# Linear attention of a two-block layer stack: two heads walked block by block, in an order fixed for TensorE

## The chip, the cores and the metric

The kernel runs on one core of one Trainium2 chip. The metric is the device time of one execution in microseconds (us). In the rows PE is TensorE's matmul, PEld its weight load, DVE is VectorE, ACT is ScalarE, POOL is GpSimd and SP is SyncE, which issues the transfers. L708 is line 708 of the kernel before.

## What is computed

The program is a stack of two blocks on 512 tokens of 1024 features: a first block with a gated linear attention (GLA) layer and a sparse attention layer, and a second block of a hybrid layer with adaptive modulation. The change touches the linear attention alone, which runs from some 20 to some 220 us. It has 4 heads with keys of 128 and values of 256, and goes over the tokens in chunks of 64 with a state:

```python
q_e = q * jnp.exp(b)              # b: running sum of the log decay in a chunk
k_e = k * jnp.exp(-b)
k_d = k * jnp.exp(b_last - b)
a = jnp.where(causal, jnp.einsum('bhnid,bhnjd->bhnij', q_e, k_e), 0.0)
o_intra = jnp.einsum('bhnij,bhnjv->bhniv', a, v)
def step(state, xs):
    o = jnp.einsum('bhcd,bhdv->bhcv', qe, state)
    state = dec[..., None] * state + jnp.einsum('bhcd,bhcv->bhdv', kd, vc)
    return state, o
...
o = rms_norm(o, head_norm)
o = o.transpose(0, 2, 1, 3).reshape(B, S, GLA_V) * jax.nn.silu(z)
return o @ w_out.astype(jnp.float32)
```

q, k, v, z and the decay's input are projections of the same normalised activations. Two small parts of other blocks are computed beside it: the modulation of the second block, `silu(c) @ w_ada`, and the table of angles for the rotary positions of the sparse attention.

## The kernel before, in words

**Tiles.** The two chunks of 64 make a block of 128 tokens; there are `NB` = 4 blocks to a head. Every projection is exact in three products of split operands: activations and weights are each a high part and a low part (`hH`, `hL`, and `w_hi`, `w_lo`), and high x high, high x low and low x high are summed. ScalarE copies out a weight's high part (L149) and VectorE makes the low part (L150), in halves of 128 x 1024; activations are split in the same way (L356, L357). A projection with features on the partitions (`proj_feat`, L236 to L238) is 24 matmuls of 512 columns; one with tokens on the partitions (`proj_toks`, L287 to L289) is 24 matmuls of 256 columns for each block of tokens.

**One head.** `gla_q` projects the queries and scales them by the decay on VectorE (L658, two halves, and L662). `gla_k` makes two scaled sets of keys, `kk` (L685, L686) and `kb` (L687, L688). `gla_v` writes the values (L605) into `gv`, one tile of [128, 4, 256] for a head, in two buffers. `gla_core` goes over the four blocks: scores (L708) go from PSUM through VectorE's copies (L711, L712) into one of two tiles `aT`, which GpSimd masks (L713); the product with the values, and with the state of the block before (L716, L718), is squared and summed on ScalarE (L720) and copied on VectorE to `on` (L721); the keys are transposed (L724), copied by ScalarE to `kt` (L726), and give the state's increment (L728, L731, L733). Behind the fourth block come the mean of squares (L736), a reciprocal root in three rounds of Newton's method on VectorE (L298 to L307, steps of 128 x 4), and GpSimd scales the four blocks of `on` by it (L739). `gla_gate` then transposes `on` (L749, 8 transposes, in two halves) and multiplies it with `silu(z)` (L745, L751).

**What lies between.** `gla_z` projects z for a head (two projections of 24 matmuls each, multiplied out at L696). `ada(n)` advances the modulation by n steps: a step issues the transfer of 512 KB of `w_ada` into one of two tiles `wada` (L548) and multiplies it on VectorE with a row sum (L549). `rope_tables` makes the angle table: steps on VectorE of 128 x 512 (L510 to L530, the later ones once for the sine and once for the cosine), then a sine on ScalarE (L531). It takes one value of `ON[2]` first (L510), and so comes no earlier than head 2's scaling.

**The order.** The heads go in two pairs (`g` = 0, 1). The code emits: queries of both heads, keys of both heads with two ada steps behind each, the whole core of the first head, two ada steps, the whole core of the second. Behind the first pair come the gates of heads 0 and 1 and the values of heads 2 and 3; behind the second pair the remaining ada steps, the z projections of heads 2 and 3, the rope table and the gates of heads 2 and 3. Then the output projection of the linear attention follows, whose input is what the gates wrote, split into `hH` and `hL` (L356, L357). In this stage the code's order is not the order on the engines: a scheduler orders the instructions of every engine, TensorE's among them, by its own estimates. Other stages of the kernel already hold TensorE to the order of the code, with `in_order(True)` (L182). An engine works through its queue in order, so what waits at the head of the queue holds up what is behind it. PSUM tiles come from four tags with 2, 3, 2 and 1 buffers:

```python
BANKS = {"pj": 2, "sc": 3, "tr": 2, "pv": 1}
```

## Time and profile before

| what | value |
|---|---|
| median of 3 runs | 1243.33 us (1241.85 to 1245.09) |
| the profiled execution's own time | 1242.91 us |
| its span in the trace | 1241.2 us |
| mean granted TensorE clock | 0.987 |
| busy: PE | 1186.5 us, 96% of the span |
| busy: DVE | 798.3 us, 64% |
| busy: ACT | 626.2 us, 50% |
| busy: POOL | 274.4 us, 22% |
| chain that ended last | PE 65%, DVE 12%, ACT 8%, issue 6%, DMA 5%, POOL 3% |

The span is the time from the first to the last recorded instruction; the execution's own time has 1.7 us more around it. Busy shares are of the whole span and say nothing of a single stage, for which the windows are read. The granted clock is the share of full speed at which TensorE was let run, and stands for two levels, 1.2 and 2.4 GHz: a stretch at 1.00 ran at the upper one. The rows of a timeline give the start, the length and the instruction; in square brackets stands the time for which the engine was idle before it, and whose work ended that time. A list of waits sums such idle times by who waited and for whom.

### The profile page before, as it was taken

What the parts mean: (1) busy time and instruction counts of PE and PEld (TensorE: products, weight loads), DVE (VectorE), ACT (ScalarE), POOL (GpSimd) and SP (SyncE); (2) the same over time, 40 slices, a digit from 0 to 9 for tenths busy, and PEclk for the clock granted to TensorE, in tenths of its full rate; (3) what the DMA queues carried; (4) which work ended last, traced back from release to release, by engine and by line L of the source; (5) the groups of instructions that cost most, each with busy time, mean ns of one, the idle gap of its engine ahead of it and who ended that gap; (6) DMA issues with size and microseconds to landing.
All of it is one profiled execution on the core that took longest, in us unless ns stands there. A gap on an engine that the chain in (4) does not pass through costs nothing.

```text
span 1241.2 us, 18591 instructions
## 1 busy us (share of the span) xinstructions
PE 1186.5 (96%) x6880; PEld 1009.8 (81%) x6880; DVE 798.3 (64%) x1534; ACT 626.2 (50%) x1308; POOL 274.4 (22%) x398
## 2 busy tenths in 40 slices
PE   6998999999989999999999999999999999999986
PEld 6788878999857777777899988988878788888776
DVE  7668888654579888776575487787666532233544
ACT  6542226754347767768676576675543222122411
POOL 2113221010004334333000186554342300000000
PEclk9999999999989999999999999999999999999988
DMA  6244645614431011111452121121242223333231
GB/s 208 68 169 144 237 121 162 200 72 133 141 112 45 8 52 35 52 35 35 152 167 74 52 85 42 61 81 57 68 153 88 99 72 99 102 102 97 86 140 51
DMA packets 39867, 122.76 MB, mean 99 GB/s; under 512 B 6352, under 2 KB 8528, under 8 KB 39136
## 3 DMA queue, kind: packets, MB, share of 16 engines
q1 hardware_dynamic: 39776, 121.57, 29.6%
q8 instruction: 54, 0.88, 0.3%
q14 instruction: 37, 0.30, 0.1%
HBM read 111.58 MB, written 6.30 MB: 95 GB/s over the span
## 4 chain that ended last, share of the span: by engine, by line
PE 65%; DVE 12%; ACT 8%; issue 6%; DMA 5%; POOL 3%; SPq 0%; DVEq 0%; ACTq 0%; POOLq 0%
PE ps_pj L236 6%; PE ps_pj L238 6%; PE ps_pj L237 6%; PE ps_tr L491 3%; PE ps_pv L1083 3%; PE ps_sc L237 3%; PE ps_sc L236 3%; PE ps_sc L238 3%; PE ps_pj L245 2%; PE ps_pj L247 2%; PE ps_pj L246 2%; DVE w_lo L150 2%; PE ps_sc L288 2%; ACT w_hi L149 2%; PE ps_sc L289 2%
## 5 line engine op out<-in xcount | busy, mean ns | idle before, releaser
L150 DVE TENSOR_TENSOR w_lo<-w_raw,w_hi 128x1024 fp32r<-128x1024 f32 (+1 forms) x154 | 189.6, 1242 | 104.8 <-ACT w_hi L149 104.3
L149 ACT CAST w_hi<-w_raw 128x1024 fp32r<-128x1024 f32 (+1 forms) x154 | 159.0, 1052 | 168.8 <-PE ps_sc L237 60.4
L236 PE MATMUL ps_pj<-hH,w_hi 128*128 128x512 f32 x512 | 206.7, 404 | 7.1 <-DVE rtm L844 4.6
L238 PE MATMUL ps_pj<-hH,w_lo 128*128 128x512 f32 x512 | 206.5, 403 | 0.0
L237 PE MATMUL ps_pj<-hL,w_hi 128*128 128x512 f32 x512 | 205.2, 401 | 0.0
L236 PEld LDWEIGHTS ps_pj<-hH,w_hi 128*128 128x128 f32 x512 | 96.8, 189 | 30.9 <-ACT w_hi L149 4.8
L1071 POOL TENSOR_SCALAR PB<-PB,sm 128x128 f32<-128x128 f32 (+3 forms) x128 | 76.8, 623 | 181.0 <-DVE sm L1067 112.5
L238 PEld LDWEIGHTS ps_pj<-hH,w_lo 128*128 128x128 f32 x512 | 96.9, 189 | 20.7 <-issue 0.5
L237 PEld LDWEIGHTS ps_pj<-hL,w_hi 128*128 128x128 f32 x512 | 96.8, 189 | 19.6 <-issue 0.2
L495 ACT CAST PTh<-ps_tr 128x512 fp32r<-128x512 f32 (+3 forms) x160 | 74.3, 481 | 67.8 <-PE ps_tr L491 65.7
L496 DVE TENSOR_TENSOR PTl<-ps_tr,PTh 128x512 fp32r<-128x512 f32 (+3 forms) x160 | 85.2, 547 | 31.8 <-ACT PTh L495 30.8
L287 PE MATMUL ps_pj<-w_hi,hH 128*128 128x256 f32 (+1 forms) x288 | 86.2, 300 | 13.8 <-ACT w_hi L577 7.5
L287 PE MATMUL ps_sc<-w_hi,hH 128*128 128x256 f32 (+1 forms) x320 | 92.0, 289 | 1.4 <-ACT w_hi L149 1.4
L288 PE MATMUL ps_sc<-w_lo,hH 128*128 128x256 f32 (+1 forms) x320 | 91.2, 285 | 0.6 <-DVE w_lo L150 0.6
L289 PE MATMUL ps_sc<-w_hi,hL 128*128 128x256 f32 (+1 forms) x320 | 90.8, 285 | 0.0
L288 PE MATMUL ps_pj<-w_lo,hH 128*128 128x256 f32 (+1 forms) x288 | 85.0, 295 | 4.5 <-DVE w_lo L150 3.3
L289 PE MATMUL ps_pj<-w_hi,hL 128*128 128x256 f32 (+1 forms) x288 | 84.4, 294 | 4.3 <-DVE hL L357 4.3
L1064 ACT ACTIVATE PB<-ps_sc,nmx 128x128 f32<-128x128 f32 (+3 forms) x128 | 66.7, 534 | 14.7 <-DVE nmx L1061 7.2
L245 PE MATMUL ps_pj<-hH,w_hi 128*128 128x512 f32 x176 | 71.1, 404 | 0.0
L247 PE MATMUL ps_pj<-hH,w_lo 128*128 128x512 f32 x176 | 69.5, 395 | 0.0
L246 PE MATMUL ps_pj<-hL,w_hi 128*128 128x512 f32 x176 | 69.2, 393 | 0.0
L287 PEld LDWEIGHTS ps_pj<-w_hi,hH 128*128 128x128 f32 x288 | 57.0, 198 | 15.0 <-ACT w_hi L577 7.5
(361 smaller groups left out, 2891.7 us busy)
## 6 DMA issues: line engine op xcount, KB each, us to landing
w_raw<-in_w_in_dram SPq DMA_DIRECT2D x64, 512.0 KB, 3.2
wada<-in_w_ada_dram SPq DMA_DIRECT2D x24, 512.0 KB, 4.1
w_raw<-in_w_nsa_dram SPq DMA_DIRECT2D x24, 512.0 KB, 3.8
w_raw<-in_w_gla_dram SPq DMA_DIRECT2D x22, 512.0 KB, 4.1
w_raw<-in_w_gla_out_dram SPq DMA_DIRECT2D x8, 512.0 KB, 3.8
w_raw<-in_w_nsa_out_dram SPq DMA_DIRECT2D x8, 512.0 KB, 3.3
w_raw<-in_w_bb_dram SPq DMA_DIRECT2D x8, 512.0 KB, 3.7
w_raw<-in_w_ba_dram SPq DMA_DIRECT2D x8, 512.0 KB, 3.6
```

The lines of the kernel that those rows point to most:

```text
L149: S.copy(hi[:, :, s], raw)
L150: lo_on[j].tensor_sub(lo[:, :, s], raw, f32(hi[:, :, s]))
L236: TE.matmul(p[:m, :tn], wh[:, k, s], aH[:, k, ts], start=(k == 0), stop=False)
L237: TE.matmul(p[:m, :tn], wh[:, k, s], aL[:, k, ts], start=False, stop=False)
L238: TE.matmul(p[:m, :tn], wl[:, k, s], aH[:, k, ts], start=False, stop=(k == KC - 1))
L245: TE.matmul(p, wh[:, k, s], aH[:, k], start=(k == 0), stop=False)
L246: TE.matmul(p, wh[:, k, s], aL[:, k], start=False, stop=False)
L247: TE.matmul(p, wl[:, k, s], aH[:, k], start=False, stop=(k == KC - 1))
L287: TE.matmul(p[:, :n], aH[:, k, s], wh[:, k, :n], start=(k == 0), stop=False)
L288: TE.matmul(p[:, :n], aH[:, k, s], wl[:, k, :n], start=False, stop=False)
L289: TE.matmul(p[:, :n], aL[:, k, s], wh[:, k, :n], start=False, stop=(k == KC - 1))
L496: V.tensor_sub(pl[:, :m], pt[:, :m], f32(ph[:, :m]))
```

## The change

- **The values** of a head are four tiles of [128, 256], one for each block, in three buffers each, where they were one tile in two buffers. The mask tiles `aT` are four, where they were two.
- **`gla_core` is cut in two.** `core_a(h, a)` is the first half of a block: scores, copies, mask, and the transposed keys. `core_b(h, a)` is the second: state, product, square, copy, and behind the last block the root and the scaling. The scaling of odd heads is done by ScalarE; that of even heads stays on GpSimd. The product of odd heads uses the PSUM tag `tr`.
- **`cores(g, fill)` walks the pair block by block.** The two heads alternate. After each half step it takes one piece of filling work, `next(fill)`: in the first pair the values of heads 2 and 3, one block of tokens to a piece (24 matmuls of 256 columns); in the second the z projections of heads 2 and 3, half a projection to a piece (12 matmuls of 512 columns). So these are no longer behind the cores.
- **Ada steps** go out two behind each query projection and one behind each `core_b`.
- **The gates of heads 0 and 1** go behind the query projections of heads 2 and 3. The rope table and the gates of heads 2 and 3 stay behind the cores of the second pair.
- **TensorE keeps the order of the code** in all of this (`in_order(True)`); the other engines are still ordered by the scheduler.

The core of the diff:

```diff
-        GV = [gp.tile([P, NB, 256], F32, tag="gv", name="gv", bufs=2) for h in range(2)]
+        GV = [[gp.tile([P, 256], F32, tag="gv%d" % b, name="gv", bufs=3) for b in range(NB)] for h in range(2)]
...
-        AT = [gp.tile([P, P], F32, name="aT%d" % i) for i in range(2)]
+        AT = [gp.tile([P, P], F32, name="aT%d" % i) for i in range(4)]
...
+        def core_a(h, a):
...
+            pa = psum("sc")
+            for b_ in range(2):
+                TE.matmul(pa[:, 64 * b_:64 * b_ + 64], kk[:, a, b_:b_ + 2].rearrange("p b i -> p (b i)"),
+                          qe[:, a, 1 - b_], start=True, stop=True)
+            aT = AT[2 * (a % 2) + h % 2]
+            V.tensor_copy(aT[0:64, 0:64], pa[0:64, 0:64])
+            V.tensor_copy(aT[:, 64:128], pa[:, 64:128])
+            G.affine_select(aT, aT, pattern=[[1, P]], compare_op=ALU.is_ge, fill=0.0, base=0,
+                            channel_multiplier=-1)
+            kt = None
+            if a < NB - 1:
+                pt = psum("tr")
+                TE.transpose(pt[:, :P], kb[:, a].rearrange("p b i -> p (b i)"), ident)
+                kt = gp.tile([P, P], F32, tag="kt", name="kt", bufs=2)
+                S.copy(kt, pt[:, :P])
+            CORE[h][3][a] = aT, kt
...
+        def core_b(h, a):
...
+            if kt is not None:
+                pst = psum("sc")
+                TE.matmul(pst[:, :256], kt, gv[a], start=True, stop=True)
+                Sn = gp.tile([P, 256], F32, tag="St%d" % (h % 2), name="St", bufs=2)
...
+            po = psum("tr" if h % 2 else "pv")
+            TE.matmul(po[:, :256], aT, gv[a], start=True, stop=(a == 0))
+            if a > 0:
+                TE.matmul(po[:, :256], qe[:, a, 1:3].rearrange("p b i -> p (b i)"), St, start=False, stop=True)
+            scr = gp.tile([P, 256], F32, tag="scr", name="scr", bufs=2)
+            S.activation(scr, po[:, :256], AF.Square, accum_out=ss[:, a:a + 1])
+            V.tensor_copy(on[:, a], po[:, :256])
+            if a == NB - 1:
...
+                y = rsqrt(ss[:], NB)
+                for a_ in range(NB):
+                    if h % 2:
+                        S.activation(on[:, a_], on[:, a_], AF.Copy, scale=y[:, a_:a_ + 1])
+                    else:
+                        G.tensor_scalar(on[:, a_], on[:, a_], y[:, a_:a_ + 1], 0.0, op0=ALU.mult, op1=ALU.add)
...
+        def cores(g, fill):
...
+            core_a(h0, 0)
+            next(fill)
+            core_a(h1, 0)
             for a in range(NB):
...
+                for h in (h0, h1):
+                    core_b(h, a)
+                    ada(1)
+                    if a < NB - 1:
+                        core_a(h, a + 1)
+                    if (h, a) != (h1, NB - 1):
+                        next(fill)
+            for _ in fill:
+                pass
...
+        def fill_v():
+            for h in (2, 3):
+                GV.append([gp.tile([P, 256], F32, tag="gv%d" % b, name="gv", bufs=3) for b in range(NB)])
+                u = unit(w_gla, 3 + h)
+                for tb in range(NB):
+                    gla_v(2, u, GV[h], (tb,))
+                    yield
...
+        def fill_z():
...
+            for h in (2, 3):
+                wh, wl = unit(w_gla, 7 + h)
+                for j in range(2):
+                    pz = psum("pj")
+                    for k in range(KC):
...
+                        if k == KC // 2 - 1:
+                            yield
+                            if (h, j) == (3, 0):
+                                yield
+                    V.tensor_mul(gz[:, 2 * h + j], pz, rT)
+                    yield
...
+        order = ExitStack()
+        order.enter_context(in_order(True))
...
                 HQ[h] = gla_q(h, uq)
+                ada(2)
+                if g:
+                    gla_gate(h - 2)
             uk = unit(w_gla, 2 + g)
             for h in hs:
                 HK[h] = gla_k(h, uk, HQ[h][1])
-                ada(2)
-            for h in hs:
-                gla_core(h, GV[h])
-                ada(2)
-            if g == 0:
-                for h in (0, 1):
-                    gla_gate(h)
...
+            cores(g, fill_z() if g else fill_v())
         ada(24)
         adas.close()
-        for h in (2, 3):
-            gla_z(h)
         rope_tables(ON[2])
         for h in range(2, 4):
             gla_gate(h)
+        order.close()
```

In the new code the lines move: scores are L711, the mask copies L714 and L715, the transposed keys L721, the state L734 to L739, the product L742 and L744, the copy L747, the mean of squares L750, the scaling L754 (ScalarE) and L756 (GpSimd), the z projection's product L800, the gates' transposes L810 and the gate L812.

TensorE, at the start of the first pair's cores, before (L708 scores, L724 transposed keys, L728 state; L287 to L289 are value matmuls of heads 2 and 3, and L238 is the end of the key projections):

```order
L238 MATMUL ps_pj<-hH,w_lo 128x512
L708 MATMUL ps_sc<-qe,kk 128x64 x2
L724 MATMUL ps_tr<-ident,kb 128x128 x2
L287 MATMUL ps_pj<-w_hi,hH 128x256
L288 MATMUL ps_pj<-w_lo,hH 128x256
L289 MATMUL ps_pj<-w_hi,hL 128x256
L287 MATMUL ps_pj<-w_hi,hH 128x256
L288 MATMUL ps_pj<-w_lo,hH 128x256
L289 MATMUL ps_pj<-w_hi,hL 128x256
L728 MATMUL ps_sc<-gv,kt 128x256
L708 MATMUL ps_sc<-qe,kk 128x64 x2
L724 MATMUL ps_tr<-ident,kb 128x128
```

And after, from the last of the 24 value matmuls that stand between head 0's scores and head 1's (L711 scores, L721 transposed keys, L734 state, L742 product):

```order
L289 MATMUL ps_pj<-w_hi,hL 128x256
L711 MATMUL ps_sc<-qe,kk 128x64 x2
L721 MATMUL ps_tr<-ident,kb 128x128
L734 MATMUL ps_sc<-gv,kt 128x256
L742 MATMUL ps_pv<-gv,aT_536 128x256
L711 MATMUL ps_sc<-qe,kk 128x64 x2
L721 MATMUL ps_tr<-ident,kb 128x128
L287 MATMUL ps_pj<-w_hi,hH 128x256
```

Before, a few value matmuls stand between the steps of one head; now a whole block of 24 stands behind a head's scores, and the other head's scores come behind them.

VectorE, ahead of the gate of head 0, before (L305 to L307 are the last round of head 0's root; L733, L711, L712 and L721 belong to head 1's core, L605 are values, L751 the gate of head 0):

```order
L733 SCALAR_TENSOR_TENSOR St<-St,db,ps_sc 128x256
L305 TENSOR_TENSOR rst<-rsy 128x4
L711 COPY aT_531<-ps_sc 64x64
L306 TENSOR_TENSOR rst<-rst,rsh 128x4
L712 COPY aT_531<-ps_sc 128x64
L307 SCALAR_TENSOR_TENSOR rsy<-rst,rsy 128x4
L605 TENSOR_SCALAR gv<-ps_pj,rc 128x256 x2
L721 COPY on<-ps_pv 128x256
L549 SCALAR_TENSOR_TENSOR wada,mod<-wada,cb 128x1024
L751 SCALAR_TENSOR_TENSOR x<-ps_tr,vec,x 128x512
```

And after (the first L307 of the `x2` is head 0's last, L658 scales the queries of head 2, L812 is the gate of head 0):

```order
L549 SCALAR_TENSOR_TENSOR wada,mod<-wada,cb 128x1024
L305 TENSOR_TENSOR rst<-rsy 128x4 x2
L549 SCALAR_TENSOR_TENSOR wada,mod<-wada,cb 128x1024
L306 TENSOR_TENSOR rst<-rst,rsh 128x4 x2
L658 SCALAR_TENSOR_TENSOR qe<-ps_pj,ex 128x4x64
L307 SCALAR_TENSOR_TENSOR rsy<-rst,rsy 128x4 x2
L658 SCALAR_TENSOR_TENSOR qe<-ps_pj,ex 128x4x64
L305 TENSOR_TENSOR rst<-rsy 128x4
L662 TENSOR_TENSOR qe<-qe,dec 128x4x64
L306 TENSOR_TENSOR rst<-rst,rsh 128x4
L307 SCALAR_TENSOR_TENSOR rsy<-rst,rsy 128x4
L305 TENSOR_TENSOR rst<-rsy 128x4
```

Head 0's root ended within head 1's core; now the roots of heads 0 and 1 run in step, and their last rounds stand around the scaling of head 2's queries.

VectorE, behind the cores of the second pair, before (L696 multiplies out a z projection, L751 is a gate, L150 a weight's low part, L357 the low part of the next stage's activations):

```order
L357 TENSOR_TENSOR hL<-x,hH 128x256 x6
L696 TENSOR_TENSOR x<-ps_pj,rT 128x512
L751 SCALAR_TENSOR_TENSOR x<-ps_tr,vec,x 128x512 x2
L150 TENSOR_TENSOR w_lo<-w_raw,w_hi 128x8x128
L751 SCALAR_TENSOR_TENSOR x<-ps_tr,vec,x 128x512 x2
L150 TENSOR_TENSOR w_lo<-w_raw,w_hi 128x8x128
L357 TENSOR_TENSOR hL<-x,hH 128x256 x8
```

And after (L521 to L530 are the rope table, L812 the gate):

```order
L523 TENSOR_SCALAR kk<-kk 128x512
L150 TENSOR_TENSOR w_lo<-w_raw,w_hi 128x8x128
L525 SCALAR_TENSOR_TENSOR rr<-kk,ang 128x512
L150 TENSOR_TENSOR w_lo<-w_raw,w_hi 128x8x128
L526 SCALAR_TENSOR_TENSOR rr<-kk,rr 128x512
L812 SCALAR_TENSOR_TENSOR x<-ps_tr,vec,x 128x512
L527 SCALAR_TENSOR_TENSOR rr<-kk,rr 128x512
L812 SCALAR_TENSOR_TENSOR x<-ps_tr,vec,x 128x512
L530 TENSOR_SCALAR rr<-rr 128x512
L521 TENSOR_SCALAR kk<-ang 128x512
L357 TENSOR_TENSOR hL<-x,hH 128x256
L522 TENSOR_SCALAR kk<-kk 128x512
```

The rope table's steps, which were done before this place, now stand between the gates of the last heads and the low parts.

## Rows read from the trace of the kernel before

**Rows 1.** Who waited for whom, TensorE, 40 to 260 us (total, times, longest):

```profile
PE ps_tr L749 <- POOL on L739: 3.0, 3, 1.1
PE ps_pj L289 <- DVE hL L357: 2.4, 1, 2.4
PE ps_pj L287 <- DVE kb L687: 2.3, 1, 2.3
PE ps_tr L724 <- DVE kb L688: 1.3, 1, 1.3
...
PE ps_pv L716 <- DVE on L721: 0.4, 1, 0.4
```

**Rows 2.** Windows around the first key wait, TensorE alone (length, busy, granted clock):

```profile
94.50:97.20 2.70, 0.41 (x5) 0.98 0.58 191
97.20:101.40 4.20, 4.20 (x18) 0.60 0.45 127
```

**Rows 3.** Timeline of VectorE before the second head's keys (start, length, engine, line):

```profile
92.80 1.81 DVE L549 SCALAR_TENSOR_TENSOR wada<-wada,cb 128x1024 f32<-128x1024 f32 x1 [1.30 <-DMA wada<-in_w_ada_dram]
...
95.69 0.68 DVE L685 TENSOR_TENSOR kk<-ps_pj,ex 128x512 f32<-128x512 f32 x1
...
96.62 0.41 DVE L687 TENSOR_TENSOR kb<-ps_pj,ex 128x256 f32<-128x256 f32 x1
```

**Rows 4.** Windows (length, busy PE, PEld, DVE, ACT, POOL, granted clock):

```profile
119.20:129.90 10.70, 10.70 (x91) 10.51 (x89) 10.02 (x27) 3.01 (x5) 1.29 (x1) 1.00 0.48 155
60.00:91.00 31.00, 31.00 (x134) 24.95 (x133) 20.21 (x29) 15.82 (x21) 4.06 (x3) 1.00 0.44 151
185.20:198.50 13.30, 13.30 (x59) 10.75 (x58) 13.20 (x37) 10.17 (x17) 3.73 (x4) 1.00 0.24 81
198.50:204.80 6.30, 3.89 (x32) 3.51 (x30) 6.30 (x10) 5.44 (x11) 0.00 (x0) 1.00 0.89 286
```

**Rows 5.** The instructions of line 739, GpSimd's scaling (ns: least, median, most):

```profile
L739 POOL TENSOR_SCALAR on<-on,rsy x16: 477/566/1564, 114.9 to 197.0; 128x256 f32<-128x256 f32 x16
```

**Rows 6.** Timelines of VectorE and GpSimd, in order of time:

```profile
144.56 0.75 DVE L658 SCALAR_TENSOR_TENSOR qe<-ps_pj,ex 128x256 f32<-128x256 f32 x2
...
180.72 2.18 POOL L739 TENSOR_SCALAR on<-on,rsy 128x256 f32<-128x256 f32 x4 [0.24 <-DVE rsy L307]
...
194.13 3.73 POOL L739 TENSOR_SCALAR on<-on,rsy 128x256 f32<-128x256 f32 x4 [11.22 <-DVE rsy L307]
```

**Rows 7.** Timelines of VectorE, ScalarE and TensorE, 180 to 207 us:

```profile
181.43 0.51 DVE L511 CAST ang<-pos_i 128x512 f32<-128x512 int32 x1
...
182.60 0.59 DVE L521 TENSOR_SCALAR kk<-ang 128x512 f32<-128x512 f32 x1
183.22 0.43 DVE L522 TENSOR_SCALAR kk<-kk 128x512 f32<-128x512 f32 x1
...
184.35 0.69 DVE L525 SCALAR_TENSOR_TENSOR rr<-kk,ang 128x512 f32<-128x512 f32 x1
...
185.32 0.39 ACT L720 ACTIVATE scr<-ps_pv 128x256 f32<-128x256 f32 x1 [2.44 <-PE ps_pv L718]
185.60 0.19 ACT L720 ACTIVATION_READ_ACCUMULATOR scr<-ps_pv 128x1 f32 x1
...
189.61 0.15 DVE L307 SCALAR_TENSOR_TENSOR rsy<-rst,rsy 128x4 f32<-128x4 f32 x1
...
198.55 1.03 PE L749 MATMUL ps_tr<-ident,on 128*128 128x128 f32 x8
199.35 1.40 DVE L751 SCALAR_TENSOR_TENSOR x<-ps_tr,vec,x 128x512 f32<-128x512 f32 x2
...
204.26 2.76 DVE L357 TENSOR_TENSOR hL<-x,hH 128x256 fp32r<-128x256 f32 x8
```

**Rows 8.** Timelines of VectorE and TensorE, the last output unit's second half:

```profile
215.31 1.23 DVE L150 TENSOR_TENSOR w_lo<-w_raw,w_hi 128x1024 fp32r<-128x1024 f32 x1 [1.43 <-ACT w_hi L149]
...
217.42 0.28 PE L287 MATMUL ps_pj<-w_hi,hH 128*128 128x256 f32 x1
```

More of the change, by code (lines that the diff above doesn't have):

```diff
@@ new lines, in core_a @@
+            kt = None
[6 more added lines that the diff above has]
+        def core_b(h, a):
+            qe, dec, db = HQ[h]
+            gv = GV[h]
+            on, ss, St, made = CORE[h]
+            aT, kt = made[a]
+            if kt is not None:
+                pst = psum("sc")
+                TE.matmul(pst[:, :256], kt, gv[a], start=True, stop=True)
+                Sn = gp.tile([P, 256], F32, tag="St%d" % (h % 2), name="St", bufs=2)
+                if a == 0:
+                    V.tensor_copy(Sn, pst[:, :256])
+                else:
+                    V.scalar_tensor_tensor(Sn, St, db[:, a:a + 1], pst[:, :256], op0=ALU.mult, op1=ALU.add)
+                CORE[h][2] = Sn
+            po = psum("tr" if h % 2 else "pv")
[6 more added lines that the diff above has]
+            if a == NB - 1:
+                V.tensor_scalar(ss, ss, 1.0 / 256, EPS, op0=ALU.mult, op1=ALU.add)
+                y = rsqrt(ss[:], NB)
+                for a_ in range(NB):
+                    if h % 2:
+                        S.activation(on[:, a_], on[:, a_], AF.Copy, scale=y[:, a_:a_ + 1])
+                    else:
+                        G.tensor_scalar(on[:, a_], on[:, a_], y[:, a_:a_ + 1], 0.0, op0=ALU.mult, op1=ALU.add)
@@ new lines, in cores @@
+        def cores(g, fill):
+            h0, h1 = 2 * g, 2 * g + 1
+            core_open(h0)
+            core_open(h1)
+            core_a(h0, 0)
+            next(fill)
+            core_a(h1, 0)
+            for a in range(NB):
+                for h in (h0, h1):
[7 more added lines that the diff above has]
+                pass
@@ new lines, in fill_v @@
+        def fill_v():
[11 more added lines that the diff above has]
+                    for k in range(KC):
+                        w_s = slice(j * P, j * P + P)
+                        TE.matmul(pz, wh[:, k, w_s], hH[:, k], start=(k == 0), stop=False)
+                        TE.matmul(pz, wh[:, k, w_s], hL[:, k], start=False, stop=False)
+                        TE.matmul(pz, wl[:, k, w_s], hH[:, k], start=False, stop=(k == KC - 1))
+                        if k == KC // 2 - 1:
[4 more added lines that the diff above has]
+                    yield
@@ L776, in tile_kernel @@
                 HK[h] = gla_k(h, uk, HQ[h][1])
-                ada(2)
-            for h in hs:
-                gla_core(h, GV[h])
-                ada(2)
-            if g == 0:
-                for h in (0, 1):
-                    gla_gate(h)
-                for h in (2, 3):
-                    gv = gp.tile([P, NB, 256], F32, tag="gv", name="gv", bufs=2)
-                    GV.append(gv)
-                    u = unit(w_gla, 3 + h)
-                    for t0 in HALVES:
-                        gla_v(h, u, gv, (t0 // P, t0 // P + 1))
-                    ada(2)
+            cores(g, fill_z() if g else fill_v())
         ada(24)
         adas.close()
-        for h in (2, 3):
-            gla_z(h)
         rope_tables(ON[2])
```

47 lines of the change are left out of this document (7 added, 40 removed).

## The prediction

> **What bounds the kernel now.** I read the page first: TensorE is busy for 96% of the span, so a change of order can win only what TensorE waits, or what it computes at the lower clock. The list of who waited for whom in the linear attention gives that amount. From 40 to 260 us TensorE waits 3.0 us for GpSimd to scale the heads before their gates, 2.4 us for the low part of the next stage's activations, 2.3 and 1.3 us for the keys of the second head of each pair, and 0.4 us for a copy [rows 1]: 9.4 us in all, under 1% of the kernel.
>
> The windows around the first key wait show a second loss. From 94.50 to 97.20 TensorE does 0.41 us of work; the 4.20 us behind it run at a granted clock of 0.60, though TensorE is busy throughout [rows 2]. At full clock that work takes 0.60 x 4.20 = 2.5 us, so the fall cost 1.7 us. What is there to win is 9.4 + 1.7 = 11.1 us.
>
> The timeline of VectorE says why the keys came late: its queue is in order, a multiplication for the adaptive weights waited 1.30 us for its transfer, and the keys stood behind it [rows 3]. The window of the tail says what covers the end of the stage now: from 185.20 to 198.50, behind the last core, TensorE is busy for 13.30 of 13.30 us, with the z projections, and VectorE for 13.20 [rows 4]. VectorE has no slack there. TensorE merely doesn't notice.
>
> **The change, part by part.** All sums start from the profiled execution, 1242.91 us; the median of the three runs is 0.4 us above it.
>
> *Keys and copies.* In the new order 24 matmuls of 256 columns (first pair) or 12 of 512 (second) stand behind each `core_a`. A 256-column matmul costs 10.70 / 91 = 0.118 us, a 512-column one 31.00 / 134 = 0.231 us [rows 4], so each piece is 2.8 us of cover. A chain of score copy, mask and product has room in that. A second L549 fills the time up to the keys, and in the new order two of them still stand ahead of the second head's keys, but the ada steps go out behind the queries instead of the keys, so their transfers start earlier. Without a late transfer the four key steps (L685 to L688) take 0.68 + 3 x 0.41 = 1.9 us [rows 3] behind their projection, under the 2.8 plus the scores: I take all 4.0 us (2.3 + 1.3 + 0.4) as won, and the 1.7 us of slow clock with them. The other bound is that the transfer is as late as now: nothing won.
>
> *Gates of heads 0 and 1.* They move behind the query projections of heads 2 and 3, which looks like cover. But in VectorE's order the last step of head 0's root (L307) stands behind an L658 that reads the query projection, which is the last thing that TensorE has to do before the gate. So after the projection TensorE waits for that matmul's end (0.28 long where the next started 0.12 behind it [rows 8], so some 0.17), L658 (0.38), L307 (0.15) [rows 6, 7] and four scalings on GpSimd. One takes 0.57 in the median [rows 5], and the four of a head took 2.2 to 3.7 us [rows 6]. With the middle, 2.9, for the four, less 0.4 of transposes that run between, this makes 3.2 us, where it was 3.0: +0.2. Bounds: 2.6 us with the median scaling, and 7 if the two L549 ahead of L658 wait for transfers as at the keys. Head 1 is scaled on ScalarE, under a projection of 24 x 0.231 = 5.5 us: covered, and worth up to 2 us if not.
>
> *The tail.* This is the large term. The z projections are now spent between the blocks; behind the last core product TensorE has 12 matmuls of z (2.8 us), 16 transposes (8 took 1.03, so 2.0) and 23 matmuls of the output projection whose operands come early (2.7): 7.5 us. What it then waits for is VectorE, on which the whole rope table, which stood between the last blocks, now stands behind them. I walk VectorE's queue from the end of the last core product, with durations from before [rows 7]; a row stands for its like (L522 for all 256-column copies and short rope steps, 0.42 to 0.43; L525 for L526 and L527 and the z product L696):
> - 1.3 us: square and its sum on ScalarE (0.39 + 0.19), the copy (0.42), and two steps of head 2's root (0.15 each).
> - to the end of head 3's root: L511 0.51, L512 and L521 0.59 each, one z product 0.69, two gates 1.40, L522 0.43, and 17 steps of four columns, 0.15 long and overlapped to some 0.09: 5.7, so 7.0.
> - ScalarE's scalings and the transposes would be done at about 9.2. But VectorE first has L523 0.43, two weight splits (2 x 1.23 [rows 8]) and two long rope steps 1.38 in its queue: 11.3.
> - two gates 1.40, L527 0.69, L530 and L521 0.42 each: 14.2. The first low part (0.42) at 14.6 lets TensorE go on; three more, each behind one rope step (0.43, 0.43, 0.69): 17.4.
>
> Neighbours that don't depend on each other start some 0.07 us before the last ends (eight L357 of 0.42 take 2.76 [rows 7]); over some 25 of them that is 1.7 us, so the tail is 15.7 to 17.4 us, and I take 16.6. TensorE is idle for 16.6 - 7.5 = 9.1 us, where it was 2.4: **+6.7**. Bounds +5 and +8.
>
> *The weights behind it.* The last output unit is split on VectorE behind those low parts. Now its second half ends at 215.31 + 1.23 = 216.5, with its first use at 217.42 [rows 8]: 0.9 us of slack. The low parts that TensorE doesn't wait for at once end about 4 us after it goes on, where they ended 204.26 + 2.76 - 204.8 = 2.2 after [rows 7]. Of the 1.8 us, 0.9 is slack: +0.9, bounds 0 and 2.
>
> *Clock.* Two gaps replace the smaller ones. Of the old ones the 2.3 us gap was followed by a stretch at the lower level, 1.2 GHz, and the 2.4 us gap before 204.8 came out of a window with clock 1.00 [rows 2, 4]. The new gate gap (3.2 us, with 8 transposes in it) and the tail's (its largest piece over 4 us) are both longer than either. I charge each with one fall at the price above: +3.4, bounds 0 and 3.4.
>
> The sum: -4.0 - 1.7 + 0.2 + 6.7 + 0.9 + 3.4 = +5.5 us, so 1248.4 in the profiled execution and **1248.8** against the median. Behind the stage the order of every engine is as before, and TensorE is the bound, so I let the delay run to the end.
>
> A rule of the Trainium skill speaks to the clock term. The page "TensorE: Matmul & The Clock Gate", section "HAM oscillation — how this bites in real kernels", tells of a kernel whose repeated waits put the engine back to half rate each time, so that each next piece starts slow. One gap here agrees (0.60 behind it) and one doesn't (1.00). By that rule the tail, made of a dozen short waits, would be at the lower level to its end; what that would cost is a rival below.
>
> **The rivals.**
> - *The tail is at its short end* and one gap alone costs clock: -5.7 + 0.2 + 5.0 + 0 + 1.7 = +1.2, so 1244.5. For it: many of the neighbours are independent. Against: VectorE's window shows no idle time that could be squeezed.
> - *Faster*: VectorE is through the rope steps before the last gate asks for it. Then the tail is the chain of square, copy, root, scaling, transposes, gate and split, some 7 us, about what TensorE has left to do, so 1 us of idle: -5.7 + 0.2 - 1.4 + 0 + 1.7 = -5.2, so 1238. This needs a tail under 10 us. Against it: the rope steps begin only when GpSimd has scaled head 2, and that head's root ends behind the last block's copy.
> - *The keys stay late*: two transfers are still ahead of them in the queue, and with buffers for two a slow one delays both. Then 2.3 + 1.3 + 1.7 come back: 1254.1. It decides from 1.5 us of lateness, the rest of the 2.8 us cover.
> - *The lower clock lasts through the tail*: its 3.9 us of transposes and early matmuls that stand between waits run at half, of which VectorE's queue hides over half: +1.7, so 1250.5.
>
> **How the numbers follow.** The forecast has 0.50, the short tail 0.22, the faster case 0.08, late keys 0.12, the lasting low clock 0.08. A difference of 0.3%, 3.7 us, is about what a measurement of this kernel can tell from none. Forecast, late keys and low clock are slower by more: 0.70; the short tail is within it: 0.22; faster 0.08. For 8 in 10 the range takes in the short tail, less 1 us for its unknown weights term, and the late keys: 1243.5 to 1254.5. It leaves out the faster case and a gate that waits for transfers on top of all.
>
> **What would show it.** Right: TensorE waits of about 3 us for GpSimd before head 0's gate and none for keys; behind the last core product some 9 us of idle in 16 to 17 us, put down to the low part L357 and to scaling; VectorE busy throughout that tail with L511 to L530. Wrong: a tail under 13 us, a gate wait under 2 us, a clock of 1.00 behind both gaps, or new waits in the middle of the blocks, for a mask or a state, which I put at nothing for 2.8 us of cover each.

## The result, and the profile after

The changed kernel takes 1251.42 us (median of 4 runs, 1249.08 to 1253.29), the kernel before 1242.67 us beside it: a ratio of 1.0073, with an interval of 1.0056 to 1.0090. It is slower by some 9 us, where +5.5 was forecast (1248.8), and its time lies within the range. Nine more runs in a later comparison (the last experiment below) gave 1.0055, interval 1.0034 to 1.0076. The sign and the size held; the terms of the sum did not, and this is the more useful half of the case.

The page of the profiled execution of after, its head and the first row of busy times (1253.29 us, the slowest of the four):

```profile
span 1251.6 us, 18572 instructions
## 1 busy us (share of the span) xinstructions
PE 1193.3 (95%) x6880; PEld 1016.0 (81%) x6880; DVE 796.6 (64%) x1534; ACT 628.9 (50%) x1315; POOL 274.0 (22%) x392
```

TensorE's busy time rose from 1186.5 to 1193.3 us with the same 6880 instructions: of the 10.4 us between the two profiled executions (spans of 1251.6 and 1241.2) 6.8 are not waiting at all, but the same work done more slowly. The mean granted clock says the same, 0.982 where it was 0.987.

Who waited for whom, TensorE from 40 to 270 us of after (total, times, longest), to be read against [rows 1]:

```profile
PE ps_pj L289 <- DVE hL L357: 4.0, 1, 4.0
PE ps_pv L742 <- POOL aT L716: 3.3, 2, 1.9
PE ps_tr L810 <- POOL on L756: 3.1, 4, 2.1
PE ps_tr L810 <- ACT on L754: 1.0, 1, 1.0
PE ps_tr L438 <- ACT ntmp L443: 0.7, 1, 0.7
PE ps_pj L288 <- DVE w_lo L150: 0.7, 1, 0.7
```

The key waits (2.3 and 1.3 us) and the copy wait are gone, as forecast. In their place stands a wait that was not: 3.3 us for GpSimd's mask, L716. The wait for the low part is longer (4.0 against 2.4). The waits for scaled heads are 4.1 in all where they were 3.0: 2.5 at head 0's gate, and 0.6 (GpSimd) and 1.0 (ScalarE) in the tail.

Windows of after, TensorE alone (length, busy, granted clock):

```profile
48.00:54.00 6.00, 6.00 (x18) 0.72 0.39 139
100.00:108.00 8.00, 6.76 (x31) 0.57 0.70 213
144.00:150.00 6.00, 5.72 (x20) 0.72 0.41 134
200.00:208.00 8.00, 6.06 (x36) 1.00 0.03 6
208.00:211.90 3.90, 0.00 (x0) 0.78 0.69 251
211.90:218.00 6.10, 6.05 (x30) 0.58 0.02 7
```

Four stretches between 40 and 240 us run at the lower level in this execution, where the kernel before had one [rows 2]. Busy time times (1 - clock) gives what each cost: 1.7, 2.9, 1.6 and 2.5 us, together 8.7.

### The profile page after: what moved, and what is told of

Same layout as the page of the kernel before. It is cut to its first block, busy times and chain, and to the rows that moved or that the text cites. A ratio compares the mean times of both kernels' runs of the same rounds, so it can differ in the third digit from the quotient of the medians.

```text
span 1251.6 us, 18572 instructions
## 1 busy us (share of the span) xinstructions
PE 1193.3 (95%) x6880; PEld 1016.0 (81%) x6880; DVE 796.6 (64%) x1534; ACT 628.9 (50%) x1315; POOL 274.0 (22%) x392
## 4 chain that ended last, share of the span: by engine, by line
PE 59%; DVE 16%; ACT 9%; DMA 6%; issue 6%; POOL 4%; SPq 0%; DVEq 0%; ACTq 0%; POOLq 0%
PE ps_pj L236 5%; PE ps_pj L238 5%; PE ps_pj L237 5%; DVE w_lo L150 3%; PE ps_tr L491 3%; PE ps_pv L1135 3%; PE ps_sc L237 3%; PE ps_sc L236 3%; PE ps_sc L238 3%; PE ps_pj L245 2%; PE ps_pj L247 2%; PE ps_pj L246 2%; ACT w_hi L149 2%; DMA wada<-in_w_ada_dram 2%; POOL us L1433 2%
## 5 line engine op out<-in xcount | busy, mean ns | idle before, releaser
L150 DVE TENSOR_TENSOR w_lo<-w_raw,w_hi 128x1024 fp32r<-128x1024 f32 (+1 forms) x154 | 190.6, 1250 | 109.7 <-ACT w_hi L149 109.4
L236 PE MATMUL ps_pj<-hH,w_hi 128*128 128x512 f32 x480 | 195.1, 406 | 7.4 <-DVE rtm L896 4.9
L238 PE MATMUL ps_pj<-hH,w_lo 128*128 128x512 f32 x480 | 193.9, 404 | 0.0
L237 PE MATMUL ps_pj<-hL,w_hi 128*128 128x512 f32 x480 | 193.6, 403 | 0.0
L287 PE MATMUL ps_pj<-w_hi,hH 128*128 128x256 f32 (+1 forms) x320 | 96.7, 303 | 11.8 <-ACT w_hi L577 8.5
L238 PEld LDWEIGHTS ps_pj<-hH,w_lo 128*128 128x128 f32 x480 | 91.5, 191 | 19.7 <-issue 0.5
L289 PE MATMUL ps_pj<-w_hi,hL 128*128 128x256 f32 (+1 forms) x320 | 95.1, 298 | 5.9 <-DVE hL L357 5.9
L288 PE MATMUL ps_pj<-w_lo,hH 128*128 128x256 f32 (+1 forms) x320 | 95.4, 298 | 5.1 <-DVE w_lo L150 3.9
L287 PE MATMUL ps_sc<-w_hi,hH 128*128 128x256 f32 (+1 forms) x288 | 82.5, 288 | 1.9 <-ACT w_hi L149 1.7
L288 PE MATMUL ps_sc<-w_lo,hH 128*128 128x256 f32 (+1 forms) x288 | 82.2, 286 | 0.6 <-DVE w_lo L150 0.6
L289 PE MATMUL ps_sc<-w_hi,hL 128*128 128x256 f32 (+1 forms) x288 | 82.0, 285 | 0.0
L287 PEld LDWEIGHTS ps_pj<-w_hi,hH 128*128 128x128 f32 x320 | 65.1, 204 | 12.8 <-ACT w_hi L577 8.5
L1116 ACT ACTIVATE PB<-ps_sc,nmx 128x128 f32<-128x128 f32 (+3 forms) x128 | 66.7, 534 | 14.2 <-DVE nmx L1113 6.7
L245 PE MATMUL ps_pj<-hH,w_hi 128*128 128x512 f32 x176 | 71.1, 404 | 0.0
L289 PEld LDWEIGHTS ps_pj<-w_hi,hL 128*128 128x128 f32 x320 | 64.9, 203 | 6.7 <-DVE hL L357 6.7
L288 PEld LDWEIGHTS ps_pj<-w_lo,hH 128*128 128x128 f32 x320 | 64.9, 203 | 6.3 <-DVE w_lo L150 4.6
```

The costliest lines, as they stand in the source:

```text
L150: lo_on[j].tensor_sub(lo[:, :, s], raw, f32(hi[:, :, s]))
L236: TE.matmul(p[:m, :tn], wh[:, k, s], aH[:, k, ts], start=(k == 0), stop=False)
L237: TE.matmul(p[:m, :tn], wh[:, k, s], aL[:, k, ts], start=False, stop=False)
L238: TE.matmul(p[:m, :tn], wl[:, k, s], aH[:, k, ts], start=False, stop=(k == KC - 1))
L245: TE.matmul(p, wh[:, k, s], aH[:, k], start=(k == 0), stop=False)
L287: TE.matmul(p[:, :n], aH[:, k, s], wh[:, k, :n], start=(k == 0), stop=False)
```

## The experiments

All are the changed kernel with the edit shown. First, how the runs are compared.

Two accounts are used below. From a trace, windows of 2 us from 40 to 240 us give the **idle time** of TensorE, and busy time times (1 - clock) summed over them gives the **clock loss** of that one execution. From all executions of a kernel, span times (1 - clock) gives the mean clock loss over the whole span, and span times clock the rest: work at full clock, and waits. The second account matters because the clock differs from one execution to the next: twelve executions of one kernel (the eleventh row) went from 1234.09 us at a clock of 0.991 to 1246.44 at 0.981, and span times clock is 1221 for both. It is not exact: where TensorE stands still at the lower level, half of the standstill counts as clock. From 40 to 240 us that is 1.3 us in the trace of after, 0.9 in that of experiment 12 (the same kernel), 0.3 in before, and 2.0 and 1.5 in experiments 2 and 3. The clocks of the four executions of before beside after are not on record; the row of before shows the three later comparisons.

| kernel | ratio to before, interval | trace: idle / clock loss | mean of runs: span x (1 - clock) | span x clock |
|---|---|---|---|---|
| before | 1 | 10.3 / 1.4 | 15.3 to 15.9 | 1224.9 to 1225.5 |
| after (4 runs) | 1.0073, 1.0056 to 1.0090 | 13.4 / 8.9 | 21.6 | 1228.0 |
| e1_rope_early | 1.0008, 0.9994 to 1.0023 | 8.2 / 3.2 | 17.3 | 1223.7 |
| e2_mask_dve | 1.0051, 1.0031 to 1.0071 | 13.5 / 6.5 | 21.0 | 1225.7 |
| e3_gate_late | 1.0037, 1.0021 to 1.0052 | 12.8 / 5.4 | 19.9 | 1225.4 |
| e4_free_order | 1.0021, 1.0006 to 1.0036 | 11.3 / 2.1 | 17.1 | 1226.1 |
| g1_rope_gate | 1.0018, 1.0001 to 1.0034 | 9.6 / 6.8 | 18.4 | 1224.1 |
| g2_rope_gate_mask | 1.0014, 1.0001 to 1.0027 | 11.2 / 5.8 | 19.3 | 1224.2 |
| g3_warm | 1.0020, 1.0003 to 1.0036 | 6.0 / 0.0 | 14.2 | 1229.4 |
| g4_z_behind | 0.9984, 0.9968 to 1.0000 | 9.3 / 4.6 | 16.8 | 1223.8 |
| h1_z_gate | 0.9975, 0.9953 to 0.9998 | 7.0 / 0.0 | 16.9 | 1221.5 |
| h2_z_gate_mask | 0.9979, 0.9961 to 0.9996 | 10.1 / 4.2 | 16.3 | 1222.2 |
| h3_ada_old | 1.0062, 1.0040 to 1.0085 | 13.6 / 8.3 | 21.5 | 1227.7 |
| h4_after_again (9 runs) | 1.0055, 1.0034 to 1.0076 | 12.7 / 5.9 | 19.3 | 1228.3 |

By the means, after lost 3 us in work and waits (1228 against 1225) and 6.1 us in clock in the first four executions, 3.4 in the nine later ones (19.3 against 15.9 in that comparison). So a half to two thirds of the loss is clock by this account, and some 0.4 to 0.6 of it if the standstill at the lower level (0.6 to 1.0 us more than before) is put with the waits. A win over after is given below as a range, against its two ratios, 1.0055 and 1.0073, of 1243 us.

### 1. The rope table ahead of the cores

```diff
+            if g:
+                rope_tables(ON[0])
             cores(g, fill_z() if g else fill_v())
...
-        rope_tables(ON[2])
```

> The changed kernel with one move: the rope table is emitted before the cores of the second pair, tied to head 0's output instead of head 2's (its integer positions share a buffer with a later temporary, to fit). Theory A, the tail on VectorE is the main loss: between the last gates and the first low part VectorE sheds nine rope steps, some 4.0 us, so TensorE's idle time behind the last core product falls from 5.9 to about 2 us, the stretch at the lower clock behind it (some 2.4 us lost) goes too, and the time is 1245 to 1246 against 1251.4. Theory B, the tail is bound by the chain of root, scaling and transposes and the losses in the blocks are the main ones: 1250 to 1251.

Measured 1242.20 us, a ratio of 1.0008: 5.8 to 8.1 us won, and no difference from the kernel before is left that could be told. Timelines of after behind the last core product (L744), VectorE, ScalarE and TensorE:

```profile
197.96 0.59 PE L744 MATMUL ps_tr<-St,qe 128*128 128x256 f32 x2
...
205.42 1.21 DVE L150 TENSOR_TENSOR w_lo<-w_raw,w_hi 128x1024 fp32r<-128x1024 f32 x1
205.44 1.70 ACT L754 ACTIVATE on<-on,rsy 128x256 f32<-128x256 f32 x4
206.56 0.68 DVE L525 SCALAR_TENSOR_TENSOR rr<-kk,ang 128x512 f32<-128x512 f32 x1
207.16 1.21 DVE L150 TENSOR_TENSOR w_lo<-w_raw,w_hi 128x1024 fp32r<-128x1024 f32 x1
208.29 0.68 DVE L526 SCALAR_TENSOR_TENSOR rr<-kk,rr 128x512 f32<-128x512 f32 x1
208.89 0.74 DVE L812 SCALAR_TENSOR_TENSOR x<-ps_tr,vec,x 128x512 f32<-128x512 f32 x1
209.56 0.68 DVE L527 SCALAR_TENSOR_TENSOR rr<-kk,rr 128x512 f32<-128x512 f32 x1
210.16 0.74 DVE L812 SCALAR_TENSOR_TENSOR x<-ps_tr,vec,x 128x512 f32<-128x512 f32 x1
210.82 0.41 DVE L530 TENSOR_SCALAR rr<-rr 128x512 f32<-128x512 f32 x1
211.15 0.41 DVE L521 TENSOR_SCALAR kk<-ang 128x512 f32<-128x512 f32 x1
211.48 0.41 DVE L357 TENSOR_TENSOR hL<-x,hH 128x256 fp32r<-128x256 f32 x1
...
211.95 0.58 PE L289 MATMUL ps_pj<-w_hi,hL 128*128 128x256 f32 x1 [3.99 <-DVE hL L357]
```

And the same place in this experiment:

```profile
198.25 0.75 DVE L812 SCALAR_TENSOR_TENSOR x<-ps_tr,vec,x 128x512 f32<-128x512 f32 x1
198.91 2.35 DVE L150 TENSOR_TENSOR w_lo<-w_raw,w_hi 128x1024 fp32r<-128x1024 f32 x2
201.17 1.41 DVE L812 SCALAR_TENSOR_TENSOR x<-ps_tr,vec,x 128x512 f32<-128x512 f32 x2
202.49 2.77 DVE L357 TENSOR_TENSOR hL<-x,hH 128x256 fp32r<-128x256 f32 x8
...
202.97 0.39 PE L289 MATMUL ps_pj<-w_hi,hL 128*128 128x256 f32 x1 [1.09 <-DVE hL L357]
```

In after VectorE goes from one instruction to the next without a gap, and five of its rope steps stand among the splits and gates ahead of the first low part. Without them TensorE waits 1.1 us where it waited 4.0. Theory A (some 6 us won) holds, at its size or somewhat over it. By the means 4.4 us of it is work and waits (1228.1 to 1223.7), the rest clock. One part of A failed: the waits of the tail are down to 0.35, 0.48 and 1.09 us, 1.9 in all, and the clock fell behind them all the same (window of TensorE in this experiment):

```profile
204.00:206.00 2.00, 2.00 (x11) 0.50 0.97 389
```

### 2. The mask on VectorE

```diff
-            V.tensor_copy(aT[0:64, 0:64], pa[0:64, 0:64])
-            V.tensor_copy(aT[:, 64:128], pa[:, 64:128])
-            G.affine_select(aT, aT, pattern=[[1, P]], compare_op=ALU.is_ge, fill=0.0, base=0,
-                            channel_multiplier=-1)
+            V.tensor_mul(aT[0:64, 0:64], pa[0:64, 0:64], tri[0:64, 0:64])
+            V.tensor_mul(aT[:, 64:128], pa[:, 64:128], tri[:, 64:128])
```

`tri` is a triangle of ones, made once ahead of the heads.

> The changed kernel with the causal mask made on VectorE: the two copies of the scores become two multiplications with a constant triangle, and GpSimd's select goes. Theory A, the select on GpSimd is stretched (2.35 and 2.29 us where it takes 0.29) while VectorE splits weights, and TensorE waits 1.9 + 1.4 us for it: both waits go, and with the first the stretch at a granted clock of 0.57 from 100 to 108 us (3.4 us lost), so 1251.4 - 6.7 = 1244.7. Theory B, the scores are late anyway because they stand behind the keys in VectorE's queue, and the clock falls as before: 1 to 2 us won, 1249.5 to 1250.5.

Measured 1248.34 us, 1.0051: 0.5 to 2.7 us won, theory B's size. The mask waits went, as A said, and the trace's idle time did not fall (13.5 us), as neither said; span times clock fell by some 2.5 (1228.1 to 1225.7), of which 0.7 to 1.1 is standstill that now counts as clock. TensorE came earlier to the gate of head 0 and waited there instead, 3.8 us in one piece, with the lower clock behind it (timeline of TensorE):

```profile
140.54 0.47 PE L812 MATMUL ps_tr<-ident,on 128*128 128x128 f32 x1 [3.81 <-POOL on L758]
```

The mechanism that A named is in the timelines of after, in order of time:

```profile
96.83 0.68 DVE L685 TENSOR_TENSOR kk<-ps_pj,ex 128x512 f32<-128x512 f32 x1
...
98.42 0.21 DVE L714 COPY aT<-ps_sc 64x64 f32<-64x64 f32 x1
...
98.69 2.34 DVE L150 TENSOR_TENSOR w_lo<-w_raw,w_hi 128x1024 fp32r<-128x1024 f32 x2
98.83 2.35 POOL L716 TENSOR_SCALAR_AFFINE_SELECT aT<-aT 128x128 f32<-128x128 f32 x1 [4.78 <-DVE aT L715]
...
101.24 1.22 PE L742 MATMUL ps_pv<-gv,aT 128*128 128x256 f32 x2 [1.92 <-POOL aT L716]
...
168.07 2.29 POOL L716 TENSOR_SCALAR_AFFINE_SELECT aT<-aT 128x128 f32<-128x128 f32 x1 [10.59 <-DVE aT L715]
...
170.60 0.29 POOL L716 TENSOR_SCALAR_AFFINE_SELECT aT<-aT 128x128 f32<-128x128 f32 x1 [0.24 <-DVE aT L715]
```

Head 0's scores were ready at 94.9, but their copy (L714) stands in VectorE's queue behind an ada step (L549), a step of the decay (L674) and the keys of head 1 (L685 and three more), so the piece of filling work was used up. Then the mask, 0.29 us long elsewhere in this trace, takes 2.35 us: it ends 0.15 us after VectorE's two splits. The Trainium skill says why that can be (page "SBUF — State Buffer", section "SBUF: two separate sides"): VectorE, in an operation with two inputs in SBUF, and GpSimd, in one that reads SBUF, share a pair of ports as an exclusive lock for whole instructions. This trace agrees: 2.35 us under two splits of 2.34 us together. That the lock is the reason was not tested by itself.

### 3. The gates of heads 0 and 1 behind the keys

```diff
                 ada(2)
-                if g:
-                    gla_gate(h - 2)
...
                 HK[h] = gla_k(h, uk, HQ[h][1])
+                if g:
+                    gla_gate(h - 2)
```

> The changed kernel with the gates of heads 0 and 1 moved from behind the query projections of heads 2 and 3 to behind their key projections. Theory A, the gate waits for head 0's root and its scaling on GpSimd: 2.5 us of waits at 143 to 144 us go, and with them the stretch at a clock of about 0.72 from 144 to 150 us (1.7 us lost), so 1251.4 - 4.2 = 1247.2. Theory B, the delay is only handed on, since VectorE's queue is full up to the keys and the cores behind: 1251 within 1 us.

Measured 1246.75 us, 1.0037: 2.2 to 4.5 us won, up to theory A's 4.2, but not by its mechanism. Timeline of TensorE in this experiment:

```profile
159.31 0.48 PE L721 MATMUL ps_tr<-ident,kb 128*128 128x128 f32 x1 [3.34 <-DVE x L812]
```

The gate's wait went, and the transposed keys wait 3.3 us for PSUM instead, which the gate of head 1 holds until VectorE multiplies it out behind the keys. The idle time of the trace is nearly the same (12.8 against 13.4), so B was right on the wait. What fell in the trace is the clock loss, 8.9 to 5.4. The two slow stretches that are missing are those at 48 and 100 us, ahead of the moved gates, and they differ between executions of one kernel too (experiment 12 and the last section), so this fall is not shown to be the edit's work. By the means span times clock fell by 2.7 (1228.1 to 1225.4), of which the trace shows 0.6 as idle time and 0.2 to 0.5 as standstill counted as clock; the rest stays open.

### 4. The scheduler orders TensorE

```diff
-        order.enter_context(in_order(True))
```

> The changed kernel without its fixed order for TensorE: the same code, and the scheduler orders TensorE like the other engines. Theory A, the loss sits in what the code asks for (where gates, z pieces and rope table stand), and the fixed order only carries it out: within 2 us of 1251.4. Theory B, the fixed order is the loss: the time goes back to 1243 to 1245.

Measured 1244.57 us, 1.0021: nearer to B. The wait for the low part stays (4.3 us in the trace) and the mask's (2.9), so what the code asks for makes the tail; but the waits for GpSimd's scaling shrank from 3.1 to 1.7 in all, and in this execution no clock fell between 40 and 200 us. The fixed order is 4.2 to 6.5 us of the loss; some 2.6 us stay without it.

### 5 and 6. Rope table early with other gates, and with the mask on VectorE

The edit of 1, the gate of head 0 behind head 2's keys, and that of head 1 behind the first scores of the pair; the sixth adds the edit of 2.

```diff
             core_a(h1, 0)
+            if g:
+                gla_gate(1)
```

> The rope table moved as in the first experiment, and the gate of head 0 behind head 2's key projection, that of head 1 behind the first scores of the second pair. If the two losses are separate, the ratio to the kernel before falls from 1.0008 by the 4.5 us that the later gates won alone: 0.997, 1238 us. If the gate's wait only moves on, as to the transposed keys in the third experiment (3.3 us), it stays at 1.000 to 1.001.

> The same with the mask made on VectorE as in the second experiment. There 2.7 us were won, and TensorE, earlier at the gate by the mask's waits, waited 4.7 us for GpSimd where it had waited 3.1. If the mask's win was handed on to that gate, it is whole here: 3.3 us of waits and the clock that falls behind some of them, so 3 to 6 us under the kernel without it: 1233 to 1235, a ratio of 0.993 to 0.995. If it was small in itself: 1 us.

Measured 1.0018 (1243.72 us) and 1.0014 (1245.79 us): nothing won over experiment 1, the second answer in both. The wait moved on as in experiment 3 (timeline of TensorE in the fifth):

```profile
168.38 0.48 PE L721 MATMUL ps_tr<-ident,kb 128*128 128x128 f32 x1 [2.87 <-DVE x L814]
```

In the sixth that wait is 3.9 us and the scores wait 3.7 us for keys. So a wait taken away in these blocks is handed to the next place where VectorE is late, because VectorE's queue is full there.

### 7. Matmuls in the gaps, to hold the clock

```diff
+        def warm(n):
+            pd = psum("sc")
+            for _ in range(n):
+                TE.matmul(pd[:, :256], ident, keep.rearrange("p c i -> p (c i)")[:, :256], start=True, stop=True)
...
+            if h == 0:
+                warm(7)
...
             gla_gate(h)
+        warm(14)
         order.close()
```

> The changed kernel with matmuls that compute nothing that is used, put where TensorE waits: 7 before head 0's gate (gap 2.1 us) and 14 behind head 3's transposes (gap 4.0 us), 256 columns each, some 0.25 us by the decay's rows (four of 512 columns take 1.98). The waits stay as they are and only the idle time goes. If the clock falls because TensorE stood still, the stretches at 144 to 150 and 212 to 218 us run at full clock, 1.1 and 2.2 us are won, and the time is 1247.5 to 1248.5. If the clock goes by something else, or those matmuls come late themselves: 1251 or more.

Measured 1244.66 us, 1.0020: 4.3 to 6.6 us won, more than the 3.3 expected, by work that is thrown away. Windows of this run at the places of the four stretches, TensorE alone, and the added matmuls in the tail:

```profile
48.00:54.00 6.00, 6.00 (x24) 1.00 0.47 150
98.00:108.00 10.00, 9.11 (x69) 1.00 0.71 211
138.00:150.00 12.00, 11.84 (x60) 1.00 0.65 218
204.00:216.00 12.00, 12.00 (x94) 1.00 0.37 113
```

```profile
199.91 6.21 PE L806 MATMUL ps_sc<-keep,ident 128*128 128x256 f32 x28
```

The clock held behind both filled gaps. The 14 matmuls took 6.2 us where some 3.5 had been estimated, so they were late themselves by about 2 us, and the mean of span times clock rose by 1.4 (1229.4); the clock loss fell by 7.4 against the first four runs of after and by 5.1 against the nine later ones. That is more than the two filled gaps cost (1.6 and 2.5 us). The two other stretches ran at full clock in this execution as well; whether by chance or because of the added work stays open.

### 8. The z projections behind the cores

```diff
-            cores(g, fill_z() if g else fill_v())
+            cores(g, iter([None] * 20) if g else fill_v())
+            if g:
+                for _ in fill_z():
+                    pass
```

> The changed kernel with the z projections of heads 2 and 3 behind the cores of the second pair again, so that nothing stands between the half steps of that pair. Theory A, the tail's cover is worth more than the cores': the tail's 5.9 us of idle time fall to 1 or less and its clock stays up, some 7 us won, against waits of up to 1 us at each of the eight half steps for mask and copy: 1244 to 1251. Theory B, the chains of the blocks are longer than the other head's work and the clock falls there: over 1252.

Measured 1242.32 us, 0.9984: 8.8 to 11 us won, theory A past its lower end. With the rope table where the change left it, the wait for the low part is 2.4 us again, as in [rows 1], and between the half steps of the second pair one wait of 1.4 us for keys is all that appears. In two points A was too hopeful: the wait in the tail fell to 2.4 us, not to 1, and the clock fell behind it in this trace (0.65 from 206 to 210 us). The z pieces covered nothing in the blocks that needed cover, and their place was in the tail.

### 9 and 10. The best order found, and the same with the mask on VectorE

The edit of 8, with head 0's gate behind both query projections and head 1's behind head 2's keys; the tenth adds the edit of 2.

```diff
                 HQ[h] = gla_q(h, uq)
                 ada(2)
-                if g:
-                    gla_gate(h - 2)
+            if g:
+                gla_gate(0)
...
                 HK[h] = gla_k(h, uk, HQ[h][1])
+                if h == 2:
+                    gla_gate(1)
```

> The z projections behind the cores as in the run before, and the gate of head 0 behind the query projections of both heads 2 and 3, that of head 1 behind head 2's keys, so that VectorE is through with them before the cores ask for their PSUM. If the gate's wait is a cost of its own: its 2.5 us of idle time and the fall of the clock behind it (140 to 143 us, some 1.5 us) go, and the ratio to the kernel before falls from 0.9984 to 0.995, 1236.5 us. If the wait is only handed on, as when the gates went behind the keys: 0.998 to 1.000.

> The same with the mask made on VectorE. Left in the run before were a mask wait of 1.9 us in the first pair with no other wait behind it to take the win. If that wait is what the select on GpSimd costs: 2 us less than without, with the clock up to 4 us, a ratio of 0.992 to 0.9935. If TensorE then only waits for VectorE (the keys and the split weights in its queue): the same as without within 1 us.

Measured 1240.26 us, 0.9975 (0.9953 to 0.9998), and 0.9979 (0.9961 to 0.9996). The ninth has the lowest ratio of the study, some 3 us under the kernel before, with an interval that ends just short of 1. The gate's wait is gone and was not handed on (waits of TensorE, 40 to 270 us):

```profile
PE ps_pj L289 <- DVE hL L357: 2.4, 1, 2.4
PE ps_pv L742 <- POOL aT L716: 1.9, 1, 1.9
PE ps_sc L711 <- DVE kk L686: 1.7, 1, 1.7
```

The win over experiment 8 is within both intervals and does not reach the 0.995 expected; span times clock fell by 2.3 us as expected (1223.8 to 1221.5), and the mean clock loss did not fall. With the mask on VectorE nothing more came: TensorE waits 5.7 us for keys there, where it waited 1.7.

### 11. The ada steps behind the keys, as before the change

```diff
                 HQ[h] = gla_q(h, uq)
-                ada(2)
...
                 HK[h] = gla_k(h, uk, HQ[h][1])
+                ada(2)
```

> The changed kernel with the two ada steps of each head behind the key projection again, where they stood before the change; all else as changed. If the filling work between the scores is what covers the second head's keys: within 2 us of the changed kernel, a ratio of 1.006 to 1.009. If the earlier transfers are what freed the keys: waits of 1 to 2 us for keys come back with their slow clock, 1.010 to 1.013.

Measured 1.0062: within the bounds of the first answer. The second head's scores wait 0.8 us for keys, and that is all that comes back of the old 3.6 (timeline of TensorE):

```profile
98.97 0.66 PE L711 MATMUL ps_sc<-qe,kk 128*128 128x64 f32 x4 [0.79 <-DVE kk L686]
```

The filling work between the scores covers the keys, not the earlier transfers.

### 12. The changed kernel again

> The changed kernel as it is, beside the others on one chip. Theory A, that two thirds of the loss is clock: 12 executions give a mean granted clock of 0.982 to 0.984 against 0.987 to 0.988 before, so 5 to 7 us of span times (1 - clock) more, and a ratio of 1.006 to 1.009. If the first four executions were unlucky in their clock: a clock of 0.985 or more and a ratio of 1.003 to 1.005.

Measured 1249.41 us, 1.0055, with a mean clock of 0.9846 and a clock loss 3.4 us over that of before. It lies on the edge between the two answers: the work and waits are the same as in the first four (1228.3 and 1228.0), and the clock differs by some 2 us between the two sets of executions.

## Why the prediction was right in sign and size, step by step

- **Keys and copies, -4.0: right.** All three waits are gone [rows 1], and experiment 11 shows that the cover, not the transfers, did it.
- **"A chain of score copy, mask and product has room in that": wrong.** This is the step that put new waits in the blocks at nothing. The copy stands behind the other head's keys in VectorE's queue, and the mask was stretched to 2.35 and 2.29 us: +3.3 us. It was named as what would prove the forecast wrong.
- **Gate of head 0, 3.2 us: nearly right.** The waits at 143 us are 2.1 + 0.4 = 2.5, 0.5 under before instead of 0.2 over it, since the four scalings took 2.1 us and not 2.9.
- **The tail, idle 9.1 us: mis-sized.** The place, the engine and the rows between were right, the length was not. One window of after, from the end of the last core product to the end of the wait (busy: PE, PEld, DVE, ACT, POOL):

```profile
198.50:211.95 13.45, 7.56 (x43) 5.54 (x42) 13.39 (x42) 8.62 (x18) 2.25 (x4) 0.93 0.22 76
```

TensorE's work is 7.56 us, as summed (7.5), but by luck: ahead of the wait stand 14 early matmuls of the output projection and not 23, and the transposes take 3.2 us and not 2.0. VectorE is busy for 13.39 of 13.45. But the idle time is 5.9 us, against 2.4 before [rows 1]: +3.5, not +6.7. The step that failed is the walk's last line: it went on to the third low part behind the first, as if TensorE stood still for each. Up to the first low part the walk has 14.6 us before its overlaps are taken off, and 13.4 were measured. TensorE went on there, and was busy from then on: 6.05 of the 6.10 us from 211.90 in the windows above, at the lower clock, behind which the further low parts came in time.
- **Weights behind, +0.9: about right**; a wait of 0.7 us for a low part of the weights is in the list.
- **Clock, +1.7 net: too small.** The trace lost 8.9 us from 40 to 240 us, where before lost 1.4: +7.5. Over all 13 runs of after it is some 4.4 us by the mean (20.0 against 15.6). Behind the gate and the tail, the two gaps charged, it was 1.6 and 2.5 us; the mask's gap took a third fall (2.9), and 48 to 54 us, before the change begins to act, a fourth (1.7) that the same kernel did not show in experiment 12.

Summed anew with what was measured: -4.0 for keys and copies, +3.3 for the mask, -0.5 for the gates (2.5 against 3.0), +3.5 for the tail and +0.7 for the weights make +3.0 us, which is what span times clock rose by (1228.0 against 1225). The clock adds 3.4 to 6.1, so 6.4 to 9.1 in all, of which 0.6 to 1.0 (the standstill at the lower level) stands in both sums. The forecast came near it because its errors had opposite signs. The rival of the lower clock had the wrong place: in the tail's three short waits (0.36, 0.29 and 1.03 us, not a dozen), 200 to 208 us, the clock was 1.00, and it fell in and behind the one gap of 4.0 us. The rule of the Trainium skill cited ahead (page "TensorE: Matmul & The Clock Gate"), as I applied it to the short waits, is not what this trace shows; that a long wait can start a slow stretch is. But in experiments 1, 5 and 6 the clock did fall among or behind the short waits of the tail, so the rule is not refuted for them. Experiment 7 shows that taking the standstill away, and not the wait, brings 4.3 to 6.6 us back.

## What to carry to other kernels

Before matmuls of a later step are used as filling, look at what they cover where they stand: here some eleven microseconds of z projections (13.3 us behind the last core product before, 2.8 after) were VectorE's cover for a table, two gates and the splits, and in the blocks they covered nothing. In these traces a long gap on TensorE cost more than its length, so price the stretch behind it and give it a chance, not a certainty. And where an engine's queue is full, as VectorE's is here, a wait taken away comes back at the next place; what lasted here were moves that took steps out of a place where TensorE waits for them (experiment 1) or gave the queue time there (8 and 9).

## What the runs showed of the hardware

- **The same gap does not always cost the clock.** The mask's wait of 1.9 us at the first block appears in seven traces. Behind it the clock fell in three (after, and experiments 5 and 12) and stayed at 1.00 in four (experiments 1, 3, 8 and 9). Windows of TensorE, first experiment, then the ninth, against 0.57 in after:

```profile
98.00:106.00 8.00, 6.83 (x54) 1.00 0.71 211
```

```profile
98.00:108.00 10.00, 8.48 (x66) 1.00 0.68 215
```

  The longer waits, ten of 3.3 to 4.3 us in eight of the traces, were each followed by a stretch at the lower level. But length alone does not decide: behind the tail's wait of 2.41 us the clock stayed at 1.00 in three traces (before, experiments 9 and 10) and fell in one (8), and in experiments 1, 5 and 6 it fell in or behind a tail with three waits of 0.35, 0.5 and 1.1 us.

- **The clock goes with most of the scatter between executions of most of these kernels.** In the ninth experiment the executions spread over 12 us, and span times clock only from 1220 to 1223 us. The fifth is an exception: there it goes from 1219 to 1229 us, over executions that spread by 8.
- **GpSimd's mask ends with VectorE's splits**: in after 0.29 us by itself, 2.35 and 2.29 us under two of them, 2.51 us under two multiplications with a row sum (L549).
